# 13 in place of 16 of the 31 convolution taps on ScalarE and GpSimd, with a third buffer for them

## The chip, the cores and the metric

The kernel runs on one core of a Trainium2 chip. Its engines are TensorE (PE in the profile; PEld is its loading of weights), VectorE (DVE), ScalarE (ACT), GpSimd (POOL) and SyncE (SP), which here only issues DMAs. Each engine takes its instructions from a queue of its own, in order; semaphores tie the queues together. The metric is the device time of one execution in microseconds (us); less is better.

## The reference

One layer of a hybrid decoder over 1024 tokens of 1024 numbers, all in float32. Half of the mixer is dilated attention in 8 heads, the other half a gated causal convolution; both go through one output projection. Then an expert layer (PEER) picks 128 of 16384 single-neuron experts for each token, and a gated embedding and a norm follow. Cut to the part that the change touches:

```python
z = xn @ w_in
q, k, v, a, gt = jnp.split(z, [D_ATTN, 2 * D_ATTN, 3 * D_ATTN, 3 * D_ATTN + D_CONV], axis=-1)
...
glu = a * jax.nn.sigmoid(gt)
c = lax.conv_general_dilated(glu, conv_w[:, None, :], window_strides=(1,),
                             padding=[(CONV_WIDTH - 1, 0)],
                             dimension_numbers=('NWC', 'WIO', 'NWC'),
                             feature_group_count=D_CONV) + conv_b
c = jax.nn.silu(_layernorm(c, conv_ln_g, conv_ln_b))
y = jnp.concatenate([_rmsnorm(attn, g_attn_out), _rmsnorm(c, g_conv_out)], axis=-1)
return y @ w_out
```

The convolution is depthwise: each of its 512 channels (`D_CONV`) is the sum of 31 earlier values of that channel (`CONV_WIDTH`), each times a weight of its own, plus a bias.

## The kernel before

The 1024 tokens lie in eight blocks of 128, and the mixer works on four groups of two blocks (256 tokens), g = 0 to 3. For each group it computes the normed input and its projections (`stage_in`), the attention and then the convolution (`stage_attend`), the output projection and the norm of the expert layer (`stage_out`), the search for the experts' keys (`stage_search`) and the combination of these into the best 128 with their gates (`stage_combine`). Blocks 0, 1, 6 and 7 then fetch their experts row by row: GpSimd issues an indirect DMA (L596), VectorE forms the product with the token for the first table (`hk`, L609) and the weighted sum for the second (`gy`, L625). These steps run spread over the whole kernel. Blocks 2 to 5 instead sweep all 128 keys on PE (`dense`, L741 to L776), after the mixer of all groups; the embedding and the last norm end the kernel. A scheduler with priorities and its own estimate of costs interleaves all this: the order of each engine's queue is not the order of the code, and a change in one place can move instructions of others.

The convolution of a group is `convolve` (L323 to L360). Its 512 channels are four tiles, c = 0 to 3, with channels on partitions and 256 tokens along them. For each tile PE forms the gate `gt` and the value `a` (L270), ScalarE the sigmoid `sg` of the gate (L331), and VectorE their product `glu` (L335), with the last 30 values of the group before it in front (L334, L337). `glu` has three buffers, so tile 3 takes that of a tile that is done. Then come the 31 taps. The first `SIDE_TAPS` go to two engines: ScalarE multiplies the shifted `glu` by the weight, the first time into `side` (L346), then into a buffer `tap` (L349), and GpSimd adds each `tap` to `side` (L350). The others go to VectorE: L353 writes the first into a sum in PSUM, `cs`, with the bias, and L356 does one multiply-add for each further tap. At last VectorE adds the two sums into `cc` (L358). `side` has two buffers, so tiles 2 and 3 begin when `cc` of tiles 0 and 1 is done; in the queues VectorE takes the taps of tiles 0 and 1 in turn, then those of 2 and 3. PE transposes `cc` back to tokens (`pc`, L423), and the layer norm of the convolution, its share of `mixed`, and the output projection follow. In names such as `cs2_3` the first number is the group, the second the channel tile; `tap1_0_14` is tap 14 of group 1, tile 0.

Other names in the rows: `r_mix` (L153) is the factor of the norm of the next group's input, `xt` (L286) its scaled input, which PE transposes (`pt_mix`, L162); `pT` (L164) is ScalarE's copy of transposed probabilities of the attention, `po` its product; `ge`, `tmp`, `step` (L557 to L566, halved in L544 to L551) belong to the combination and are bf16; `ya` is the output of the attention, `sqj_ya` its sum of squares on ScalarE.

Of the kernel before, what the change touches and what calls it, by code (L numbers as in the profile page):

```python
# [10 lines left out]
F32 = mybir.dt.float32  # L11
# [9 lines left out]
P = 128  # L21
# [8 lines left out]
GN = GT * P  # L30
# [7 lines left out]
DC = 512  # L38
NCT = DC // P
TAPS = 31  # L40
SIDE_TAPS = 16
ROT = 8
PH = 8
TOPK = 16
# [57 lines left out]
def tile_layer(ctx, tc, t, consts, out):  # L102
# [18 lines left out]
    def scope(parent, **kw):  # L121
        s = parent.enter_context(ExitStack())
        return s, s.enter_context(tc.tile_pool(bufs=1, **kw))
# [8 lines left out]
    att, apool = scope(ctx, name="apool", side="right")  # L132
# [132 lines left out]
    def channel_major(xT, w_k, c0, name):  # L265

        w = w_piece(w_k[c0], f"w_{name}").rearrange("p (k c) -> p k c", k=KD)
        a = lin(name)[:, : xT.shape[2]]
        for k in range(KD):
            nc.tensor.matmul(a, w[:, k, :], xT[:, k, :], start=k == 0, stop=k == KD - 1)  # L270
        return a
# [52 lines left out]
    def convolve(g, xT):  # L324

        gn = xT.shape[2]
        glus = []
        for c in range(NCT):
            pg = channel_major(xT, w_ag, NCT + c, f"gt{g}_{c}")
            sg = mpool.tile([P, GN], F32, tag="t2", name=f"sg{g}_{c}", bufs=3)[:, :gn]  # L330
            S.activation(sg, pg, AF.Sigmoid)  # L331
            pa = channel_major(xT, w_ag, c, f"a{g}_{c}")
            glu = apool.tile([P, TAPS - 1 + GN], F32, tag="glu", name=f"glu{g}_{c}", bufs=NCT - 1)[:, : TAPS - 1 + gn]
            V.tensor_copy(glu[:, 0 : TAPS - 1], last[:, c, :])  # L334
            V.tensor_tensor(glu[:, TAPS - 1 :], pa, sg, ALU.mult)  # L335
            if g + 1 < NG:
                V.tensor_copy(last[:, c, :], glu[:, gn:])  # L337
            glus.append(glu)
        cT = []
        for c, glu in enumerate(glus):  # L340
            tap = lambda k: (glu[:, k : k + gn], cw[:, c, k : k + 1])
            side = apool.tile([P, GN], F32, tag="side", name=f"side{g}_{c}", bufs=2)[:, :gn]
            for k in range(SIDE_TAPS):
                xk, wk = tap(k)
                if k == 0:
                    S.activation(side, xk, AF.Copy, scale=wk)  # L346
                else:
                    m = apool.tile([P, GN], F32, tag="tap", name=f"tap{g}_{c}_{k}", bufs=2)[:, :gn]
                    S.activation(m, xk, AF.Copy, scale=wk)  # L349
                    G.tensor_tensor(side, side, m, ALU.add)  # L350
            sums = lin(f"cs{g}_{c}")[:, :gn]
            xk, wk = tap(SIDE_TAPS)
            V.tensor_scalar(sums, xk, wk, cw[:, c, TAPS : TAPS + 1], ALU.mult, ALU.add)  # L353
            for k in range(SIDE_TAPS + 1, TAPS):
                xk, wk = tap(k)
                V.scalar_tensor_tensor(sums, xk, wk, sums, ALU.mult, ALU.add)  # L356
            cc = apool.tile([P, GN], F32, tag="cc", name=f"cc{g}_{c}", bufs=5)[:, :gn]
            V.tensor_tensor(cc, sums, side, ALU.add)  # L358
            cT.append(cc)
        return cT  # L360
# [474 lines left out]
    def stage_attend(g):  # L835
        qT, xT = st[g]
        ys = attend(g, qT)
        st[g] = (ys, convolve(g, xT))
# [143 lines left out]
```

## Time and profile before

| | us |
|---|---|
| Median of 3 runs | 3184.26 |
| Lowest and highest | 3178.24, 3186.3 |
| Profiled execution | 3174.52 |
| Span of its instructions | 3172.8 |
| PE busy | 2723.0 |
| VectorE busy | 2487.8 |
| GpSimd busy | 1551.7 |
| ScalarE busy | 1154.2 |

The profile is of one execution. Its span runs from the first to the last instruction; the execution's own time is 1.7 us longer. "Busy" counts the time in which an engine had an instruction in work. The mean TensorE clock granted over the span was 0.939 of full speed. By stretches of time, the four mixers fill the first 1040 us, the work of the last group's search and combination follows, and the sweep over all keys runs from about 1455 to 3050 us.

A line of the timeline gives when a run of equal instructions starts, how long it lasts, the engine, the line of the code, the operation, what is written and read, the shapes and the number of instructions. In brackets stands how long the engine was idle before it and which instruction ended that idle time.

### The profile page before, as it was taken

What the parts mean: (1) busy time and instruction counts of PE and PEld (TensorE: products, weight loads), DVE (VectorE), ACT (ScalarE), POOL (GpSimd) and SP (SyncE); (2) the same over time, 40 slices, a digit from 0 to 9 for tenths busy, and PEclk for the clock granted to TensorE, in tenths of its full rate; (3) what the DMA queues carried; (4) which work ended last, traced back from release to release, by engine and by line L of the source; (5) the groups of instructions that cost most, each with busy time, mean ns of one, the idle gap of its engine ahead of it and who ended that gap; (6) DMA issues with size and microseconds to landing.
All of it is one profiled execution on the core that took longest, in us unless ns stands there. A gap on an engine that the chain in (4) does not pass through costs nothing. (4 is left out here: it accounts for less than half of the span.)

```text
span 3172.8 us, 36112 instructions
## 1 busy us (share of the span) xinstructions
PE 2723.0 (86%) x11711; PEld 1994.6 (63%) x11711; DVE 2487.8 (78%) x5116; ACT 1154.2 (36%) x2129; POOL 1551.7 (49%) x1268
## 2 busy tenths in 40 slices
PE   6588938986995677996999999999999999999996
PEld 3455614853574365665777777777777777777643
DVE  1428867997897799886889889888888888888851
ACT  3623453264345327882222222222222222232342
POOL 0500685466546531215556556566556566655620
PEclk9799969988998788997999999999999999999998
DMA  5154849845954664989999999999999999999840
GB/s 164 54 168 135 313 161 376 313 159 196 354 199 153 255 255 129 283 264 346 339 338 331 332 339 361 342 347 343 334 331 346 343 339 361 335 329 333 324 169 24
DMA packets 304528, 865.76 MB, mean 273 GB/s; under 512 B 26778, under 2 KB 93746, under 8 KB 304338
## 3 DMA queue, kind: packets, MB, share of 16 engines
q0 software_dynamic: 147456, 536.94, 46.4%
q1 hardware_dynamic: 153616, 323.16, 29.4%
q10 hardware_dynamic: 3266, 3.36, 0.4%
q8 instruction: 92, 1.51, 0.2%
q14 instruction: 98, 0.80, 0.1%
HBM read 819.83 MB, written 43.52 MB: 272 GB/s over the span
## 5 line engine op out<-in xcount | busy, mean ns | idle before, releaser
L596 POOL DMA_INDIRECT u<-in_expert_u_dram,ex x512 | 674.1, 1317 | 812.1 <-DVE hk L609 539.4
L596 POOL DMA_INDIRECT v<-in_expert_v_dram,ex x512 | 692.4, 1352 | 494.7 <-DVE gy L625 362.9
L625 DVE SCALAR_TENSOR_TENSOR gy<-v,ga,gy 128x1024 f32<-128x1024 f32 x512 | 657.5, 1284 | 41.8 <-DMA v<-in_expert_v_dram,ex 33.0
L609 DVE CUSTOM_DVE_ANT_0 u<-u,gxn 128x1024 f32<-128x1024 f32 x512 | 613.7, 1226 | 57.9 <-DMA u<-in_expert_u_dram,ex 57.7
L741 PE MATMUL ph<-xh,uh 128*128 128x512 f32 x1024 | 404.5, 395 | 42.5 <-DMA gt<-gate_d 29.0
L743 PE MATMUL ph<-xh,ul 128*128 128x512 f32 x1024 | 407.2, 398 | 23.6 <-DVE ul L719 23.4
L742 PE MATMUL ph<-xl,uh 128*128 128x512 f32 x1024 | 402.6, 393 | 0.0
L759 ACT CAST vh<-v 128x1024 fp32r<-128x1024 f32 x128 | 131.5, 1051 | 736.8 <-PE kept_y L774 491.2
L350 POOL TENSOR_TENSOR side<-side,tap 128x256 f32<-128x256 f32 x240 | 184.9, 771 | 183.6 <-ACT tap L349 135.1
L741 PEld LDWEIGHTS ph<-xh,uh 128*128 128x128 f32 x1024 | 194.5, 190 | 89.2 <-ACT uh L717 49.8
L743 PEld LDWEIGHTS ph<-xh,ul 128*128 128x128 f32 x1024 | 194.1, 190 | 79.3 <-DVE ul L719 39.3
L772 PE MATMUL py<-vh,ah 128*128 128x512 f32 x512 | 204.4, 399 | 43.8 <-ACT ah L751 43.8
L761 DVE TENSOR_TENSOR vl<-v,vh 128x1024 fp32r<-128x1024 f32 x128 | 153.8, 1222 | 110.2 <-ACT vh L759 110.1
L270 PE MATMUL pq<-x2T,w_pq 128*128 128x256 f32 x1024 | 230.4, 383 | 5.7 <-DMA w_pq<-in_peer_wq_dram 5.3
L742 PEld LDWEIGHTS ph<-xl,uh 128*128 128x128 f32 x1024 | 194.5, 190 | 41.7
L270 PEld LDWEIGHTS pq<-x2T,w_pq 128*128 128x128 f32 x1024 | 193.7, 192 | 34.6 <-issue 4.5
L773 PE MATMUL py<-vl,ah 128*128 128x512 f32 x512 | 200.4, 395 | 0.0
L774 PE MATMUL kept_y<-vh,al 128*128 128x512 f32 x512 | 199.4, 390 | 0.0
L772 PE MATMUL kept_y<-vh,ah 128*128 128x512 f32 x512 | 199.3, 389 | 0.0
L773 PE MATMUL kept_y<-vl,ah 128*128 128x512 f32 x512 | 199.2, 389 | 0.0
L774 PE MATMUL py<-vh,al 128*128 128x512 f32 x512 | 198.8, 395 | 0.0
L717 ACT CAST uh<-u 128x1024 fp32r<-128x1024 f32 x128 | 134.1, 1048 | 108.0 <-DMA u<-in_uT_dram 78.9
(264 smaller groups left out, 4685.2 us busy)
## 6 DMA issues: line engine op xcount, KB each, us to landing
u<-in_uT_dram SPq DMA_DIRECT2D x128, 512.0 KB, 6.9
v<-in_expert_v_dram SPq DMA_DIRECT2D x128, 512.0 KB, 6.5
w_pq<-in_peer_wq_dram SPq DMA_DIRECT2D x64, 512.0 KB, 5.8
gate_d<-stage SPq DMA_DIRECT2D x16, 2048.0 KB, 11.5
gt<-gate_d SPq DMA_DIRECT2D x64, 512.0 KB, 10.8
w_o<-in_w_out_dram SPq DMA_DIRECT2D x32, 512.0 KB, 5.8
w_k<-in_w_qkv_dram SPq DMA_DIRECT2D x16, 512.0 KB, 5.0
w_q<-in_w_qkv_dram SPq DMA_DIRECT2D x16, 512.0 KB, 4.3
```

What stands on the lines that cost most here:

```text
L270: nc.tensor.matmul(a, w[:, k, :], xT[:, k, :], start=k == 0, stop=k == KD - 1)
L350: G.tensor_tensor(side, side, m, ALU.add)
L596: d = G.indirect_dma_start(out=e, out_offset=None, in_=table, in_offset=bass.IndirectOffsetOnAxis(ap=index, axis=0))
L609: uses(V.tensor_tensor_reduce(out=e, in0=e, in1=xn, scale=1.0, scalar=0.0, op0=ALU.mult, op1=ALU.add, accum_out=hk[:, k : k + 1]))
L625: uses(V.scalar_tensor_tensor(y, e, act[:, k : k + 1], y, ALU.mult, ALU.add))
L741: nc.tensor.matmul(ph, hi, xh[:, k, :], start=k == 0, stop=False)
L742: nc.tensor.matmul(ph, hi, xl[:, k, :], start=False, stop=False)
L743: nc.tensor.matmul(ph, lo, xh[:, k, :], start=False, stop=k == KD - 1)
L761: V.tensor_tensor(b, v, a.bitcast(F32), ALU.subtract)
L772: nc.tensor.matmul(py, ah[e][:, rows(j)], vh[e][:, half(f)], start=first, stop=False)
L773: nc.tensor.matmul(py, ah[e][:, rows(j)], vl[e][:, half(f)], start=False, stop=False)
L774: nc.tensor.matmul(py, al[e][:, rows(j)], vh[e][:, half(f)], start=False, stop=last_e)
```

## The change

`SIDE_TAPS` goes from 16 to 13, the buffers of `tap` from two to three, and those of `cc` from five to four. For each channel tile ScalarE now multiplies 13 taps and GpSimd adds 12; VectorE takes 18, one by L353 and 17 by L356, where it was 15, one and 14. Each `tap` and each `cc` buffer holds 256 float32 numbers per partition, so the two pools together need as much memory as before.

```diff
-SIDE_TAPS = 16
+SIDE_TAPS = 13
...
-                    m = apool.tile([P, GN], F32, tag="tap", name=f"tap{g}_{c}_{k}", bufs=2)[:, :gn]
+                    m = apool.tile([P, GN], F32, tag="tap", name=f"tap{g}_{c}_{k}", bufs=3)[:, :gn]
...
-            cc = apool.tile([P, GN], F32, tag="cc", name=f"cc{g}_{c}", bufs=5)[:, :gn]
+            cc = apool.tile([P, GN], F32, tag="cc", name=f"cc{g}_{c}", bufs=4)[:, :gn]
```

The counts alone do not tell the order of the queues, which the scheduler makes anew. Three places differ in more than the number of taps.

The first is VectorE at the end of the convolution of group 2. Before, the queue held:

```order
L356 SCALAR_TENSOR_TENSOR cs2_3_4204<-glu2_3_3958,cw_91,cs2_3_4204 128x256
L358 TENSOR_TENSOR cc2_2_4155<-cs2_2_4139,side2_2_4092 128x256
L356 SCALAR_TENSOR_TENSOR cs2_3_4204<-glu2_3_3958,cw_91,cs2_3_4204 128x256
L563 TENSOR_TENSOR tmp2_4289<-ge2_4283,step2_4286 128x2048
L356 SCALAR_TENSOR_TENSOR cs2_3_4204<-glu2_3_3958,cw_91,cs2_3_4204 128x256
L544 TENSOR_TENSOR tmp2_4289<-tmp2_4289 128x128x8
L356 SCALAR_TENSOR_TENSOR cs2_3_4204<-glu2_3_3958,cw_91,cs2_3_4204 128x256
L566 TENSOR_TENSOR ge2_4283<-ge2_4283,cb16_87 128x2048
L358 TENSOR_TENSOR cc2_3_4220<-cs2_3_4204,side2_3_4157 128x256
L544 TENSOR_TENSOR ge2_4283<-ge2_4283 128x128x8
L153 RECIPROCAL r_mix3_4415<-sd_mix3_4413 128x2
L153 RECIPROCAL r_ya2_4617<-sd_ya2_4615 128x2
```

and now it holds:

```order
L356 SCALAR_TENSOR_TENSOR cs2_2_4070<-glu2_2_3882,cw_91,cs2_2_4070 128x256
L356 SCALAR_TENSOR_TENSOR cs2_3_4129<-glu2_3_3910,cw_91,cs2_3_4129 128x256
L358 TENSOR_TENSOR cc2_2_4089<-cs2_2_4070,side2_2_4032 128x256
L358 TENSOR_TENSOR cc2_3_4148<-cs2_3_4129,side2_3_4091 128x256
L557 TENSOR_TENSOR ge2_4211<-ge2_4211,cb16_87 128x2048
L153 RECIPROCAL r_mix3_4343<-sd_mix3_4341 128x2
L153 RECIPROCAL r_ya2_4545<-sd_ya2_4543 128x2
L563 TENSOR_TENSOR tmp2_4217<-ge2_4211,step2_4214 128x2048
L334 COPY glu3_0_5683<-last_100 128x30
L334 COPY glu3_1_5710<-last_100 128x30
L544 TENSOR_TENSOR tmp2_4217<-tmp2_4217 128x128x8
```

The operations of the combination (`tmp2`, `ge2`), which lay between the last taps of tile 3, now come behind `cc2_3`; one of them, L557, lies between it and `r_mix3`.

The second is ScalarE in the convolution of group 1, where tiles 0 and 1 end. Before, these rows stood among the taps of tiles 0 and 1:

```order
L349 ACTIVATE tap1_0_14_2368<-glu1_0_2239,cw_91 128x256
L151 ACT_TABLE_LOAD
L151 ACTIVATE sd_mix2_2596<-ssq_mix2_2591,eps_89 128x2
L349 ACTIVATE tap1_0_15_2371<-glu1_0_2239,cw_91 128x256
L349 ACTIVATE tap1_1_1_2394<-glu1_1_2267,cw_91 128x256
L146 ACTIVATE sqj_ya1_0_2794,ssq_ya1_2793<-ya2_2071 128x512
L349 ACTIVATE tap1_1_2_2397<-glu1_1_2267,cw_91 128x256
L349 ACTIVATE tap1_1_3_2400<-glu1_1_2267,cw_91 128x256
L146 ACTIVATE sqj_ya1_1_2796,ssq_ya1_2793<-ya3_2213 128x512
L349 ACTIVATE tap1_1_4_2403<-glu1_1_2267,cw_91 128x256
L349 ACTIVATE tap1_1_5_2406<-glu1_1_2267,cw_91 128x256
L151 ACTIVATE sd_ya1_2798<-ssq_ya1_2793,eps_89 128x2
```

and `side1_2` came later, right behind the last of those taps and the first two of tile 2. Now the same operations follow the last tap of tile 1:

```order
L349 ACTIVATE tap1_1_11_2394<-glu1_1_2243,cw_91 128x256
L349 ACTIVATE tap1_1_12_2397<-glu1_1_2243,cw_91 128x256
L349 ACTIVATE tap1_2_1_2423<-glu1_2_2271,cw_91 128x256
L349 ACTIVATE tap1_2_2_2426<-glu1_2_2271,cw_91 128x256
L349 ACTIVATE tap1_2_3_2429<-glu1_2_2271,cw_91 128x256
L151 ACT_TABLE_LOAD
L151 ACTIVATE sd_mix2_2548<-ssq_mix2_2543,eps_89 128x2
L146 ACTIVATE sqj_ya1_0_2746,ssq_ya1_2745<-ya2_2047 128x512
L146 ACTIVATE sqj_ya1_1_2748,ssq_ya1_2745<-ya3_2189 128x512
L151 ACTIVATE sd_ya1_2750<-ssq_ya1_2745,eps_89 128x2
L346 ACTIVATE side1_2_2421<-glu1_2_2271,cw_91 128x256
L346 ACTIVATE side1_3_2480<-glu1_3_2299,cw_91 128x256
```

The table load, `sd_mix2`, the two `sqj_ya1` and `sd_ya1` now lie between the last tap of tile 1 and `side1_2`.

The third is ScalarE in the convolution of group 3, around the last sigmoid `sg3_3`. Before:

```order
L349 ACTIVATE tap3_1_12_5939<-glu3_1_5782,cw_91 128x256
L349 ACTIVATE tap3_1_13_5942<-glu3_1_5782,cw_91 128x256
L349 ACTIVATE tap3_1_14_5945<-glu3_1_5782,cw_91 128x256
L331 ACTIVATE sg3_3_5823<-gt3_3_5814 128x256
L146 ACTIVATE sqj_ya3_0_6283,ssq_ya3_6282<-ya6_5467 128x512
L146 ACTIVATE sqj_ya3_1_6285,ssq_ya3_6282<-ya7_5729 128x512
```

and now, where tile 1 had its last taps between the heads of the attention (`sb7` and `pT7` are those of block 7):

```order
L349 ACTIVATE tap3_1_12_5861<-glu3_1_5710,cw_91 128x256
L386 ACTIVATE sb7_7_5623,den7_5398<-sb7_7_5623,nm7_7_5624 128x1024
L164 COPY pT7_6_4_5612<-pt_p7_6_4_0_5613 128x512
L331 ACT_TABLE_LOAD
L331 ACTIVATE sg3_2_5724<-gt3_2_5715 128x256
L164 COPY pT7_7_0_5633<-pt_p7_7_0_0_5634 128x512
L556 COPY ge4_6064<-p164_6062 128x2048
L164 COPY pT7_7_4_5644<-pt_p7_7_4_0_5645 128x512
L349 ACTIVATE tap3_2_1_5887<-glu3_2_5737,cw_91 128x256
L349 ACTIVATE tap3_2_2_5890<-glu3_2_5737,cw_91 128x256
L349 ACTIVATE tap3_2_3_5893<-glu3_2_5737,cw_91 128x256
L331 ACTIVATE sg3_3_5751<-gt3_3_5742 128x256
```

The taps 4 to 14 of `tap3_1`, which stood in one row between the last `pT7` copy and `sg3_3` (the last three are shown), have moved ahead among the copies; three taps of tile 2 stand ahead of `sg3_3` now. On VectorE the combination's `tmp4` and the three operations that follow it (L544, L566, L544) come behind `cc3_3`, where before they lay ahead of the taps.

## Rows read from the trace of the kernel before

**Rows 1.** The page's first part: busy us (share of the span) and instructions by engine.
```profile
PE 2723.0 (86%) x11711; PEld 1994.6 (63%) x11711; DVE 2487.8 (78%) x5116; ACT 1154.2 (36%) x2129; POOL 1551.7 (49%) x1268
```

**Rows 2.** Busy us (instructions) by stretch: PE, PEld, DVE, ACT, POOL; clock, DMA share, GB/s.
```profile
700.00:738.00 38.00, 0.17 (x1) 0.00 (x0) 28.33 (x71) 21.01 (x43) 25.43 (x32) 0.54 0.14 51
...
1098.00:1170.00 72.00, 68.28 (x330) 57.85 (x330) 62.20 (x252) 11.56 (x27) 35.45 (x28) 0.97 0.87 328
...
1455.00:2950.00 1495.00, 1414.90 (x6058) 1139.98 (x6058) 1309.24 (x1720) 400.44 (x514) 894.33 (x640) 0.99 0.93 338
...
3051.00:3173.00 122.00, 89.91 (x230) 44.43 (x228) 21.26 (x33) 34.31 (x70) 0.00 (x0) 0.86 0.09 33
```

**Rows 3.** Tile `side`: durations in ns (min/median/max), then who waited: us, times.
```profile
L350 POOL TENSOR_TENSOR side<-side,tap x240: 716/725/1802, 91.4 to 1038.1; 128x256 f32<-128x256 f32 x120
...
  ACT tap L349: 78.0, 179
...
  DVE cc L358: 51.9, 9
```

**Rows 4.** Tile `cs`: what its engine sat idle for: us, times.
```profile
  ACT sg L331: 15.4, 3
```

**Rows 5.** Timeline, first convolution: start us, duration us, operation, [idle before <-releaser].
```profile
104.27 16.71 POOL L350 TENSOR_TENSOR side<-side,tap 128x256 f32<-128x256 f32 x21 [1.64 <-ACT tap L349]
...
112.64 3.62 PE L270 MATMUL gt<-xT,w_gt 128*128 128x256 f32 x16
...
121.82 0.55 DVE L353 TENSOR_SCALAR cs<-glu,cw 128x256 f32<-128x256 f32 x1 [6.80 <-ACT sg L331]
...
134.69 23.89 POOL L350 TENSOR_TENSOR side<-side,tap 128x256 f32<-128x256 f32 x30 [13.71 <-ACT side L346]
...
158.61 0.42 DVE L358 TENSOR_TENSOR cc<-cs,side 128x256 f32<-128x256 f32 x1 [11.48 <-POOL side L350]
```

**Rows 6.** Timeline, second convolution.
```profile
402.12 1.28 ACT L151 ACT_TABLE_LOAD   x1
...
406.10 0.61 ACT L146 ACTIVATE sqj_ya<-ya 128x512 bf16<-128x512 f32 x1
...
416.94 0.42 DVE L358 TENSOR_TENSOR cc<-cs,side 128x256 f32<-128x256 f32 x1 [6.41 <-POOL side L350]
...
417.92 23.86 POOL L350 TENSOR_TENSOR side<-side,tap 128x256 f32<-128x256 f32 x30 [1.02 <-ACT side L346]
...
418.17 11.05 DVE L356 SCALAR_TENSOR_TENSOR cs<-glu,cw,cs 128x256 f32<-128x256 f32 x28
...
429.91 0.42 DVE L358 TENSOR_TENSOR cc<-cs,side 128x256 f32<-128x256 f32 x1 [0.69 <-POOL side L350]
...
441.82 0.42 DVE L358 TENSOR_TENSOR cc<-cs,side 128x256 f32<-128x256 f32 x1 [11.48 <-POOL side L350]
...
443.55 1.12 PE L162 MATMUL pt_mix<-cst,xt 128*128 128x128 f32 x4 [47.01 <-ACT xt L286]
```

**Rows 7.** Timeline, third convolution.
```profile
710.40 26.14 POOL L350 TENSOR_TENSOR side<-side,tap 128x256 f32<-128x256 f32 x30 [8.75 <-ACT side L346]
...
723.12 1.22 DVE L563 TENSOR_TENSOR tmp<-ge,step 128x2048 bf16<-128x2048 bf16 x1
...
737.51 0.16 DVE L153 RECIPROCAL r_mix<-sd_mix 128x2 f32<-128x2 f32 x1
...
738.90 1.12 PE L162 MATMUL pt_mix<-cst,xt 128*128 128x128 f32 x4 [38.73 <-ACT xt L286]
```

**Rows 8.** Timeline, fourth convolution.
```profile
990.88 3.62 PE L270 MATMUL gt<-xT,w_gt 128*128 128x256 f32 x16
...
991.85 9.42 POOL L350 TENSOR_TENSOR side<-side,tap 128x256 f32<-128x256 f32 x9
...
1002.11 0.55 DVE L353 TENSOR_SCALAR cs<-glu,cw 128x256 f32<-128x256 f32 x1 [5.79 <-ACT sg L331]
```

**Rows 9.** The page's fifth part, the gather's second half: xcount | busy us, mean ns | idle.
```profile
L625 DVE SCALAR_TENSOR_TENSOR gy<-v,ga,gy 128x1024 f32<-128x1024 f32 x512 | 657.5, 1284 | 41.8 <-DMA v<-in_expert_v_dram,ex 33.0
```

## The prediction, made before the change was run

> **What bounds the kernel now.** I began with busy time by engine [rows 1]. TensorE leads with 86%, VectorE has 78%, GpSimd 49%, ScalarE 36%: no engine sets the end alone, so the next view is busy time by stretch [rows 2]. From 1455 to 2950 us, the sweep over all keys, PE is busy 1414.90 of 1495.00 us at a granted clock of 0.99; 3051 to 3173 is PE's tail. Both are PE's, and no convolution lies in them: all sixteen channel tiles (four groups of tokens, four tiles each) are done by 1039 us. In that front part PE waits. In 700 to 738 us it works 0.17 of 38.00 us, at a mean clock of 0.54 (near the lower of its levels, 1.2 of 2.4 GHz), while VectorE works 28.33 and GpSimd 25.43. That stretch is the end of a convolution.
>
> The third view is who waits for the side sums [rows 3]: VectorE stood idle 51.9 us in nine places, before adding `side` to its own sum, until GpSimd's last add. The tile of VectorE's sums shows a second wait, 15.4 us in three places, for the sigmoid `sg` on ScalarE [rows 4]. These are what the change can reach; the rest of the front waits for other things.
>
> The fourth view is the timeline at the four convolutions. VectorE does tiles 0 and 1 together ("pair 1"), then 2 and 3 ("pair 2"). In pair 2 of the second convolution GpSimd's 30 adds take 23.86 us, 0.795 each, and VectorE's 28 fused taps 11.05 us, 0.395 each [rows 6]. VectorE then waits 11.48 us, PE waits with it, and the transposes of the next group come only behind it, after 47.01 us of idle PE. Here a tap taken from GpSimd costs half as much on VectorE, and VectorE has the room. Is ScalarE the limit instead? No: its multiplies are shorter than an add, and the 30 adds stand in one unbroken row. So the third `tap` buffer, and the ScalarE time saved, are worth nothing in pair 2.
>
> **The change part by part.** GpSimd loses 3 adds in each of 16 tiles: 48 x 0.795 = 38.2 us. ScalarE loses 48 multiplies. VectorE gains 48 taps: 48 x 0.395 = 19.0 us. Of that, 24 taps lie in the four pairs 2, under GpSimd, which needs 24 x 0.795 = 19.1 us there against about 14.4 for VectorE (34 x 0.395 and two first taps). Thus each pair 2 shortens by 6 x 0.795 = 4.8 us and VectorE keeps some 4.5 us of idle time. What pair 1 does differs by convolution.
>
> First convolution [rows 5]. In pair 1 VectorE waits 6.80 us for the sigmoid of tile 3, which stands on ScalarE among the taps of tile 1, and these run at GpSimd's pace: GpSimd's 21 adds end at 104.27 + 16.71 = 120.98. With six adds fewer they end at 104.27 + 15 x 0.796 = 116.2. The gate's product is on PE until 112.64 + 3.62 = 116.26, so the sigmoid cannot start before that, and VectorE's start moves from 121.82 to about 117.2: 4.6 us earlier, less 6 x 0.395 = 2.4 for its own added taps, 2.2 net. With pair 2, **-6.9** (rounded down from 7.0).
>
> Second convolution [rows 6]. Pair 1 ends with a wait of 6.41 us for GpSimd, at 416.94. GpSimd's adds would end 4.8 us earlier or more; VectorE's own taps end 2.4 later, at about 412.4, so the end is about 412.8, 4.1 earlier. But the order on ScalarE changes: the table load, the norm of the next tokens and the two of `ya` (1.28 us and three or four pieces of 0.3 to 0.6) come behind pair 1's last tap, ahead of `side1_2`, where before they lay among the taps. I take 2 us late from it. 4.1 + 4.8 - 2 = **-7.1** (bounds -6 and -9).
>
> Third convolution [rows 7]. Pair 2's 30 adds take 26.14 us, not 23.9, because three operations of the search's combination on two bf16 inputs (1.22 us for `tmp`, and two like it) run on VectorE beside them. After the change they stand behind the last `cc`, but for one of 1.2 us ahead of `r_mix3`. The pair starts 0.5 us later (2.4 for its own taps, less what the shorter tile 0 gives back), takes 19.1, and pays the 1.2: 710.9 + 19.1 + 0.4 + 1.2 = 731.8 for `r_mix3` against 737.5, **-5.7**. At the worst VectorE, which has the 3 to 4 us of deferred work and 2.4 of taps still to do, gives all but 0.4 of it back in the next stage; at best -7.
>
> Fourth convolution [rows 8]. Before, the sigmoid of tile 3 stood behind eleven taps of tile 1, and VectorE waited 5.79 us, starting at 1002.11; the gate's product ends on PE at 994.5. In the new order those taps lie earlier, between the heads of the attention, so VectorE may start at about 995.0. 34 x 0.395 then puts pair 1's end 4.6 us earlier; pair 2 gives 4.8: -9.4. Two costs stand against it. ScalarE's copies of the probabilities (`pT7`) now have up to three taps between them and PE waits for those copies: twelve taps of 0.5 us, mostly in gaps, for which I take +2 (bounds 0 and +10, if each tap waits for its add behind a gather fetch). And four bf16 operations (3.8 us) with three more gather steps (3 x 1.28 = 3.9 [rows 9]) reach VectorE between this convolution and the sweep; from 1040 on VectorE has idle time (62.20 of 72.00 busy in 1098 to 1170 [rows 2]), so I take +2.5 of at most +7.7. Sum **-4.9**.
>
> Sweep and tail: 0, since PE sets both [rows 2] and nothing in its work there changes; a few gather steps move by two places under 1309.24 us of VectorE. The fifth buffer of `cc` goes, and costs nothing: a group has four, and the next group's first comes 150 us or more after its transposes.
>
> The sum is -6.9 - 7.1 - 5.7 - 4.9 = -24.6 us. The profiled execution took 3174.52 us, 1.7 more than its span and 9.7 under the median of the runs shown, 3184.26. 3174.52 - 24.6 = 3149.9; on the median, 3159.7, which I call **3159**.
>
> One rule speaks against the change. In pair 2 of the second convolution the first 15 adds ran beside VectorE's taps (417.92 to 429.91, 12.0 us) and the last 15 while VectorE stood idle (to 441.82, 11.9 us) [rows 6]: the taps do not slow GpSimd. The third convolution's adds beside bf16 operations did slow, to as much as 1.80 us [rows 3, 7]. The Trainium skill, "SBUF — State Buffer", section "Who interferes with whom", says that a VectorE instruction with two SBUF inputs contends with a GpSimd instruction that reads SBUF, and one with at most one SBUF input does not. The taps have one input in SBUF and one in PSUM, the bf16 operations two in SBUF, and the trace agrees on both. By that rule the taps that move are free of contention, and my sum would stay.
>
> **The rivals.**
>
> *GpSimd's adds slow down* (slower). After the change VectorE works through 14.4 of pair 2's 19.1 us, before 12.0 of 23.9. If more of VectorE's work beside them stretches the adds, as in the nine adds of 9.42 us at 991.85 (1.047 each [rows 8]), pair 2 takes 24 x 1.047 = 25.1 us, 1.2 longer than now; with 2.4 on VectorE in pair 1 that is +3.6 in each convolution, +14.4 in all: about **3199**. It decides from 0.896 us per add ((23.9 - 2.4) / 24). Against it stands the equal pace of the two halves above. The Trainium skill's "Perfetto Trace Analysis", section "Optimizing Scalar/DVE Operations", advises the opposite of this change (work off a saturated VectorE, on to ScalarE or even GpSimd); with VectorE idle in pair 2 the trace does not bear that out. Chance 0.05.
>
> *The gain is lost behind the convolutions* (little change). Attention 7 is held up by the taps among its copies (+10 in place of +2), the deferred work of the fourth convolution lies wholly on the path (+7.7 in place of +2.5), and the third gives back all but 0.4. Then -24.6 + 8 + 5.2 + 5.3 = -6.1: about **3178**, within the noise. For it speaks that VectorE is the busiest engine around these places; against it, that 28.33 of 38.00 us in the third tail leave it idle time. Chance 0.14.
>
> *The third buffer gives more.* In pairs 1 of the third and fourth convolutions adds alternate with gather fetches, and ScalarE's queue, which also holds PE's copies, waits for adds. With a tap more of slack ScalarE stands less often: -35 to -40, about **3147**. Nothing in the rows prices it beyond the 78 us that ScalarE waited in all. Chance 0.15.
>
> *It does not do what it says.* If the convolution's end did not release PE, nothing would move: 3184. The wait of 11.48 us before the last `cc`, with PE idle for 47.01 us and released by the instruction behind it [rows 6], speaks against it. Chance 0.02.
>
> **How the numbers follow.** Forecast (about -13 to -33 us) 0.64, more gain 0.15, lost gain 0.14, slower 0.05, nothing 0.02. The range leaves out the slower rival, the flat cases' far end and the far end of the large gain: 3143 to 3176. A measurement of this kernel can tell 0.3%, about 9.5 us, from no change. Faster by more than that: 0.64 + 0.15 = 0.79 and a little of the lost-gain case, 0.80. Within it: 0.14, less that, and 0.02: 0.15. Slower: 0.05.
>
> **What would show it.** In the new trace VectorE's wait for GpSimd before `cc` should fall from 51.9 us to about 18 (four times 4.5); the wait for the sigmoid from 15.4 to a few; pair 2 should be an unbroken row of 24 adds in 19.1 us; the idle PE before the transposes of the next tokens should fall from 47.01 by about 7 and in the third convolution from 38.73; and the sweep should keep its length of 1495 us but start near 1430. I am wrong if adds take over 0.9 us in pair 2, if attention 7 grows by more than the fourth convolution gives, or if the sweep or PE's tail changes by more than 5 us.

## The result and the profile after

The changed kernel took 3154.72 us (median of 4 runs, 3145.36 to 3160.1) against 3185.28 us for the kernel before (4 runs beside it). That is 30.6 us faster; the forecast was 3159 with a range of 3143 to 3176. The ratio of the runs on record is 0.9912, interval 0.9889 to 0.9935 (that of the two medians is 0.9904). Three later comparisons, on two chips, gave 0.9936 (0.9918 to 0.9955), 0.9963 (0.995 to 0.9976) and 0.9938 (0.9916 to 0.9961): the change gains 0.4 to 0.9%, some 20 us in the mean of the four. Single executions of the changed kernel spread from 3145 to 3178 us. The profiled one took 3160.1 us, so the difference of two profiled executions (14.4 us) says less than the stages in them.

The busy time of the changed kernel, against [rows 1]:

```profile
PE 2740.0 (87%) x11711; PEld 2003.6 (63%) x11711; DVE 2504.5 (79%) x5164; ACT 1132.6 (36%) x2082; POOL 1487.7 (47%) x1220
```

VectorE has 16.7 us more in 48 more instructions, GpSimd 64 us less. Next, who waits around the tiles `side` and `cs` (durations in ns; then us, times), against [rows 3, 4]:

```profile
L350 POOL TENSOR_TENSOR side<-side,tap x192: 718/727/1803, 91.0 to 1011.0; 128x256 f32<-128x256 f32 x192
...
  DVE cc L358: 21.2, 4
...
  ACT sg L331: 8.3, 2
```

VectorE's wait for GpSimd fell from 51.9 us in nine places to 21.2 in four, its wait for the sigmoid from 15.4 to 8.3. The timeline of the first convolution (start us, duration us, operation, [idle before <-releaser]), against [rows 5]:

```profile
117.47 0.55 DVE L353 TENSOR_SCALAR cs<-glu,cw 128x256 f32<-128x256 f32 x1 [3.59 <-ACT sg L331]
...
132.69 19.12 POOL L350 TENSOR_TENSOR side<-side,tap 128x256 f32<-128x256 f32 x24 [16.07 <-ACT side L346]
...
133.30 13.40 DVE L356 SCALAR_TENSOR_TENSOR cs<-glu,cw,cs 128x256 f32<-128x256 f32 x34
...
151.84 0.42 DVE L358 TENSOR_TENSOR cc<-cs,side 128x256 f32<-128x256 f32 x1 [4.82 <-POOL side L350]
```

Pair 1 starts at 117.47, where it was 121.82. Pair 2 is one unbroken row of 24 adds in 19.12 us beside 34 taps in 13.40; VectorE still waits 4.82 us, not 11.48. The second convolution, against [rows 6]:

```profile
406.88 0.41 DVE L358 TENSOR_TENSOR cc<-cs,side 128x256 f32<-128x256 f32 x1
...
408.32 0.61 ACT L146 ACTIVATE sqj_ya<-ya 128x512 bf16<-128x512 f32 x1
...
409.83 19.10 POOL L350 TENSOR_TENSOR side<-side,tap 128x256 f32<-128x256 f32 x24 [4.16 <-ACT side L346]
...
428.97 0.43 DVE L358 TENSOR_TENSOR cc<-cs,side 128x256 f32<-128x256 f32 x1 [6.71 <-POOL side L350]
...
430.70 1.11 PE L162 MATMUL pt_mix<-cst,xt 128*128 128x128 f32 x4 [41.32 <-ACT xt L286]
```

Pair 1 no longer waits for GpSimd. Pair 2's first add waits 4.16 us for `side1_2`, which stands behind the two `sqj_ya` on ScalarE; the idle PE before the transposes fell from 47.01 to 41.32 us. The third and the fourth, against [rows 7, 8]:

```profile
699.68 19.10 POOL L350 TENSOR_TENSOR side<-side,tap 128x256 f32<-128x256 f32 x24 [15.12 <-ACT side L346]
...
718.81 0.42 DVE L358 TENSOR_TENSOR cc<-cs,side 128x256 f32<-128x256 f32 x1 [4.79 <-POOL side L350]
...
721.68 1.12 PE L162 MATMUL pt_mix<-cst,xt 128*128 128x128 f32 x4 [31.93 <-ACT xt L286]
...
973.70 3.24 PE L270 MATMUL gt<-xT,w_gt 128*128 128x256 f32 x14
...
976.98 0.38 ACT L331 ACTIVATE sg<-gt 128x256 f32<-128x256 f32 x1 [2.45 <-issue]
...
992.62 19.11 POOL L350 TENSOR_TENSOR side<-side,tap 128x256 f32<-128x256 f32 x24 [14.45 <-ACT side L346]
...
1011.76 0.42 DVE L358 TENSOR_TENSOR cc<-cs,side 128x256 f32<-128x256 f32 x1 [4.89 <-POOL side L350]
```

The last `cc` starts at 1011.76 us. Before, it was this row:

```profile
1038.90 0.42 DVE L358 TENSOR_TENSOR cc<-cs,side 128x256 f32<-128x256 f32 x1 [11.48 <-POOL side L350]
```

27.1 us are gained there, and 14.4 of them reach the end of the program. How the stages compare in all the traces of the two programs, each stage in us from one mark of the timeline to the next (the start of the last `cc` of each convolution, the start of the first product of the sweep on L741, the end of its last product on L774, the start of the last instruction, which issues the output's DMA):

| Stage | Before, 2 traces | Changed, 4 traces | Difference of means | Forecast |
|---|---|---|---|---|
| to the first convolution's end | 158.6, 159.8 | 151.8, 153.4, 152.4, 153.7 | -6.4 | -6.9 |
| to the second's | 283.2, 284.6 | 277.1, 276.1, 274.3, 274.1 | -8.5 | -7.1 |
| to the third's | 294.8, 294.2 | 289.8, 291.9, 290.9, 283.7 | -5.4 | -5.7 |
| to the fourth's | 302.3, 304.4 | 293.0, 303.2, 298.1, 300.3 | -4.7 | -7.4 |
| to the sweep | 416.0, 418.7 | 426.2, 423.3, 422.8, 428.1 | +7.7 | +2.5 |
| sweep | 1515.8, 1519.2 | 1519.4, 1518.1, 1522.6, 1523.3 | +3.4 | 0 |
| tail | 198.4, 198.4 | 197.3, 195.9, 198.2, 197.6 | -1.1 | 0 |

The gains of the first three convolutions and the loss behind the fourth stand in every trace. The stage to the fourth convolution spreads over 10 us in one program. All of that spread lies ahead of the last taps: from the end of the last gate product on PE (before 990.88 + 3.62 = 994.50, changed 973.70 + 3.24 = 976.94) to the last `cc` it takes 44.4 us in both traces of before and 34.8 in all four of the changed kernel.

### The profile page after: what moved, and what is told of

Its sections match the earlier page's. It is cut to its first block, busy times and chain, and to the rows that moved or that the text cites. A ratio compares the mean times of both kernels' runs of the same rounds, so it can differ in the third digit from the quotient of the medians.

```text
span 3158.3 us, 36012 instructions
## 1 busy us (share of the span) xinstructions
PE 2740.0 (87%) x11711; PEld 2003.6 (63%) x11711; DVE 2504.5 (79%) x5164; ACT 1132.6 (36%) x2082; POOL 1487.7 (47%) x1220
## 5 line engine op out<-in xcount | busy, mean ns | idle before, releaser
L596 POOL DMA_INDIRECT u<-in_expert_u_dram,ex x512 | 654.4, 1278 | 830.1 <-DVE hk L609 568.0
L596 POOL DMA_INDIRECT v<-in_expert_v_dram,ex x512 | 682.3, 1333 | 513.0 <-DVE gy L625 380.6
L741 PE MATMUL ph<-xh,uh 128*128 128x512 f32 x1024 | 407.1, 398 | 44.0 <-ACT uh L717 43.9
L741 PEld LDWEIGHTS ph<-xh,uh 128*128 128x128 f32 x1024 | 195.8, 191 | 91.8 <-ACT uh L717 51.9
L350 POOL TENSOR_TENSOR side<-side,tap 128x256 f32<-128x256 f32 x192 | 150.8, 787 | 194.6 <-ACT tap L349 133.6
L742 PEld LDWEIGHTS ph<-xl,uh 128*128 128x128 f32 x1024 | 195.9, 191 | 42.0
L774 PE MATMUL kept_y<-vh,al 128*128 128x512 f32 x512 | 199.7, 390 | 0.0
L774 PE MATMUL py<-vh,al 128*128 128x512 f32 x512 | 198.3, 395 | 0.3 <-DVE al L753 0.3
```

Of the source, the lines that this page charges most:

```text
L596: d = G.indirect_dma_start(out=e, out_offset=None, in_=table, in_offset=bass.IndirectOffsetOnAxis(ap=index, axis=0))
L741: nc.tensor.matmul(ph, hi, xh[:, k, :], start=k == 0, stop=False)
L742: nc.tensor.matmul(ph, hi, xl[:, k, :], start=False, stop=False)
L774: nc.tensor.matmul(py, al[e][:, rows(j)], vh[e][:, half(f)], start=False, stop=last_e)
```

## The experiments

**Was the first pair of traces chance?** Both kernels as they are, once more each.

> The changed kernel once more, for a second trace and a narrower ratio. In the first pair of traces the four convolutions ended 27.1 us earlier, but the program only 14.4 us earlier: 10.1 us went between the last convolution and the sweep, where the output projection of the last group waited for its weights (w_o) by DMA. Theory 1 (the loss belongs to the new order: three more gather steps, each with a fetch of 512 KB, lie in that stage): this trace shows the same loss, the last cc about 27 us earlier than before and the sweep's first product 16 to 18 us earlier; ratio 0.990 to 0.993. Theory 2 (the loss was chance of one execution, since the medians lie 30 us apart): the sweep starts 22 to 28 us earlier than before.

> The kernel before once more, for a second trace: how far the times of the stages (last cc, first and last product of the sweep, end) differ between two executions of one program. If the stages repeat within 2 us up to the sweep, and the sweep itself differs by several us, the spread of the runs (3178 to 3188) is made in the sweep, not in the convolutions.

Measured: ratio 0.9936 and, in the second trace of before, 1043.05 us for the last `cc` and 1461.77 for the sweep's first product. The stages of before repeat within 2.7 us up to the sweep, where I had expected 2, and within 3.5 in it. The changed kernel's second trace has the loss behind the fourth convolution again (423.3), so the loss belongs to the new order, as theory 1 has it; which part of the order makes it is asked below. The other numbers of theory 1 missed: against the second trace of before the last `cc` came 18.5 us earlier and the sweep 13.8, not 27 and 16 to 18. The last `cc` came at 1024.59, not 1011.76, and 10 us of that lie in the stage to the fourth convolution, in the attention of the last group. Busy us (instructions) by stretch (PE, PEld, DVE, ACT, POOL; clock, DMA share, GB/s), first of the first trace:

```profile
909.00:918.50 9.50, 8.35 (x46) 5.71 (x47) 9.50 (x54) 7.28 (x16) 8.23 (x10) 1.00 0.04 12
...
918.30:927.30 9.00, 9.00 (x54) 6.40 (x54) 8.62 (x66) 5.21 (x11) 2.84 (x4) 1.00 0.23 65
```

and of the second, for the same work:

```profile
913.00:922.50 9.50, 8.57 (x46) 5.52 (x44) 9.50 (x54) 7.26 (x17) 7.85 (x9) 1.00 0.09 34
...
923.00:940.10 17.10, 17.10 (x53) 11.85 (x54) 8.98 (x66) 6.13 (x12) 2.86 (x4) 0.50 0.18 57
```

The order is the same and PE is full in both, but the same products take 9.00 us in the first trace and 17.10 in the second, where PE runs at its lower level (0.50, 1.2 of 2.4 GHz). That is 8 of the 10 us. Just before it the two traces are alike: PE was busy 8.35 and 8.57 of 9.50 us at 1.00. Of the twelve other traces of this study, four have such a stretch with PE full in this attention (10 to 17 us), and one, that of the taps alone (below), has 10.2 us with PE busy in 9.50 of them; the changed kernel's third and fourth and the two of before have none. What brings it on stays open.

**Which part of the change works?** The taps alone and the buffers alone.

```diff
# taps_only, against the kernel before
-SIDE_TAPS = 16
+SIDE_TAPS = 13
# buffer_only, against the changed kernel
-SIDE_TAPS = 13
+SIDE_TAPS = 16
```

> 13 side taps, with two tap buffers and five cc buffers as before. If the gain is GpSimd's three fewer adds in each tile, and the third buffer is worth nothing: pair 2 is 24 adds of 0.796 us, the last cc of the fourth convolution 23 to 28 us earlier than before, and the time equals the changed kernel's within 0.3%. Here VectorE's queue keeps the combination's bf16 operations inside the third convolution, which costs 2 to 3 us there, but only 18 gather steps lie between the last convolution and the next norm, as before, not 21, so that the loss in that stage should be smaller by theory 1: sweep 20 to 28 us earlier. If the third buffer carries the gain (ScalarE waits less for adds): 10 us or less faster than before.

> 16 side taps as before, with three tap buffers and four cc buffers. If the buffer is worth nothing in itself: 30 adds still take 23.9 us in pair 2 and the time is within 0.3% of before. The order of VectorE's queue changes with it (two of the bf16 operations leave the third convolution), which may give 2 us there. If the buffer carries the gain: 15 us or more faster.

Measured, beside the changed kernel's 0.9936 on the same chip: taps alone 0.9961 (0.9941 to 0.998), buffers alone 1.0032 (1.0015 to 1.005), some 10 us slower than before, which neither expectation had. With 13 taps the third buffer adds some 7 us of gain (the intervals overlap, so this is likely and not settled), with 16 it costs 10. It does nothing to the adds: 24 of them took 19.07 us with two buffers. With taps alone the last `cc` came at 1031.90, 7.0 and 11.1 us earlier than in the two traces of before, not 23 to 28: in this trace the attention of the last group took longer (10.2 us of it at the lower clock), and a wait is back. What the buffer changes is the order. The fourth convolution with taps alone:

```profile
997.17 0.36 ACT L331 ACTIVATE sg<-gt 128x256 f32<-128x256 f32 x1
...
997.57 0.55 DVE L353 TENSOR_SCALAR cs<-glu,cw 128x256 f32<-128x256 f32 x1 [5.79 <-ACT sg L331]
...
1012.80 19.07 POOL L350 TENSOR_TENSOR side<-side,tap 128x256 f32<-128x256 f32 x24 [14.97 <-ACT side L346]
```

Here nine multiplies of tile 1 stand ahead of `sg3_3` on ScalarE, as eleven did before the change, and VectorE waits 5.79 us for it, as in [rows 8]. In the changed kernel they lie among the attention's heads and that wait is gone. The sweep came 417.2 us behind the last `cc`, as in before: 21 gather steps lie there up to the first product of the next search, 22 in before, 25 in the changed kernel. With the buffers alone the order is disturbed too, and to no use:

```profile
422.25 23.90 POOL L350 TENSOR_TENSOR side<-side,tap 128x256 f32<-128x256 f32 x30 [4.16 <-ACT side L346]
...
714.91 24.99 POOL L350 TENSOR_TENSOR side<-side,tap 128x256 f32<-128x256 f32 x30 [9.88 <-ACT side L346]
...
727.67 1.22 DVE L557 TENSOR_TENSOR ge<-ge,cb 128x2048 bf16<-128x2048 bf16 x1
...
1029.82 25.00 POOL L350 TENSOR_TENSOR side<-side,tap 128x256 f32<-128x256 f32 x30 [14.44 <-ACT side L346]
```

In the second convolution the first add waits 4.16 us for a `side1_2` that the same ScalarE work precedes as in the changed kernel, and no shorter pair pays for it. VectorE no longer waits for the last sigmoid here either. The rest of this trace's loss lies mostly in the last group's attention, where 20 us run at the lower clock, which by the 17.10 and 9.00 us above costs some 10 (an estimate). One trace does not explain a median of twelve runs; their granted clock was lower as well, 0.9335 in the mean against 0.9372 in the 23 runs of before beside them, and what lowers it is not shown. The two buffer counts were always changed together, so the runs do not tell them apart.

**Where do the 8 us behind the last convolution go?** The gather's steps on VectorE held back there, with their fetches.

```diff
-        V.reciprocal(r, sd)
+        marks[name] = V.reciprocal(r, sd).ins.name
...
-            uses(V.scalar_tensor_tensor(y, e, act[:, k : k + 1], y, ALU.mult, ALU.add))
+            uses(gy := V.scalar_tensor_tensor(y, e, act[:, k : k + 1], y, ALU.mult, ALU.add)); order_after(gy.ins, marks["ffn3"]) if (i, k) == (FEW[0], 104) else None
```

> The changed kernel, in which the 104th row of the first gathered block is used on VectorE only after the norm behind the last output projection (r_ffn3): five gather steps lie between the last convolution and that norm, not 21, and the fetches of 512 KB behind them wait too. All else keeps its order up to the last cc. If the gain of the convolutions is lost in that stage to the gather's rows, which share the DMA engines with the weights w_o: from the last cc to the sweep's first product 410 to 416 us, in place of 426 and 423, and the time 6 to 14 us under the changed kernel's. If the loss comes from VectorE's deferred bf16 operations or from a lower clock by chance: the stage stays at 420 or more and the time is the same. If the gather's rows are on the path anyway: the sweep and its tail get longer by what the stage gains, and the time is the same.

The output projection of the last group, from the last `cc` to the first product of the search, in before, in the changed kernel and in this one:

```profile
1039.00:1099.40 60.40, 41.00 (x102) 19.47 (x103) 53.52 (x79) 22.71 (x41) 27.52 (x21) 0.81 0.73 258
```

```profile
1011.80:1084.40 72.60, 47.00 (x102) 21.10 (x103) 61.62 (x86) 22.83 (x41) 29.75 (x24) 0.78 0.70 249
```

```profile
1024.40:1081.50 57.10, 41.34 (x102) 19.31 (x103) 44.12 (x71) 22.83 (x41) 11.22 (x8) 0.83 0.55 183
...
1081.50:1444.40 362.90, 288.07 (x1642) 208.01 (x1641) 300.21 (x797) 215.74 (x518) 88.01 (x79) 0.88 0.74 239
```

60.40, 72.60 and 57.10 us, with 22, 25 and 10 gather steps. PE's waits in it, in the changed kernel and in this one:

```profile
1047.92 1.98 PE L261 MATMUL o<-w_o,yT 128*128 128x512 f32 x4 [2.64 <-DMA w_o<-in_w_out_dram]
...
1052.42 2.70 PE L261 MATMUL o<-w_o,yT 128*128 128x512 f32 x4 [2.52 <-DMA w_o<-in_w_out_dram]
...
1067.48 5.24 PE L261 MATMUL o<-w_o,yT 128*128 128x512 f32 x8 [3.79 <-DMA w_o<-in_w_out_dram]
```

```profile
1041.56 3.39 PE L261 MATMUL o<-w_o,yT 128*128 128x512 f32 x4 [3.96 <-DMA w_o<-in_w_out_dram]
...
1051.33 19.35 PE L261 MATMUL o<-w_o,yT 128*128 128x512 f32 x42
```

One wait for the weights `w_o` is left, of 3.96 us; behind it 42 products run in one row. VectorE's bf16 operations, which this kernel has in the same place, do not make the stage long by themselves: the gather's steps are needed for it. But holding them back takes two things out of the stage at once, VectorE's time for them (busy 44.12 us, not 61.62) and their fetches (183 GB/s, not 249), so this run does not tell which of the two costs. The other traces, between the same two marks, do not settle it either (us; the last column is PE's waits for `w_o`):

| Kernel | Gather steps | Stage | VectorE busy | `w_o` waits |
|---|---|---|---|---|
| before, 2 traces | 22 | 60.4, 62.2 | 53.5, 53.8 | 7.0, 5.9 |
| taps alone | 21 | 59.9 | 53.2 | 5.5 |
| changed, 4 traces | 25 | 72.6, 70.5, 69.8, 69.1 | 61.7 in each | 8.9, 9.6, 10.6, 11.3 |
| steps held back | 10 | 57.1 | 44.1 | 4.0 |
| buffers alone | 20 | 64.9 | 53.0 | 10.5 |
| 11 taps (below) | 19 | 63.8 | 51.6 | 10.7 |
| 9 taps (below) | 19 | 67.6 | 51.5 | 8.4 |
| 16 taps in the fourth (below) | 20 | 65.7 | 53.1 | 10.8 |

From before to the changed kernel VectorE's busy time grew by 8 us, and the stage by 9; PE's waits for weights grew by some 4. The last four kernels have fewer steps than before and no more work on VectorE, and yet they wait longer for weights and take longer. So the number of steps alone does not set it. They share the third `tap` buffer with the changed kernel, and with it another order; what in that order delays the weights stays open.

The stage behind, up to the sweep, takes 362.90 us here, against 353.6 in the changed kernel's first trace (352.9 to 359.1 in the others), and the time is 0.9932 (0.99 to 0.9963), the changed kernel's within the noise. The whole came out at 420 us, not at the 410 to 416 of the first expectation. The steps held back take their time further on, as in the third expectation, but ahead of the sweep and not in the sweep and its tail, where I had put it.

**Is 13 the best number, and when does VectorE become the bound?** `SIDE_TAPS` 11 and 9, the rest as changed.

> 11 side taps, three tap and four cc buffers. Pair 2: GpSimd 20 x 0.796 = 15.9 us, VectorE 38 x 0.395 and two first taps and a cc = 16.4 us, so that both end together; 3 us less than with 13. Pair 1: 4 x 0.395 = 1.6 us more on VectorE. Net 1.4 us less in each convolution, and 15 gather steps, not 21, in the last output projection, worth some 5 us: 5 to 11 us faster than the changed kernel. If VectorE is already the bound of the front with 13: 16 to 25 us slower than it (64 taps more at 0.395 over both).

> 9 side taps. Pair 2 is now bound by VectorE: 42 x 0.395 + 1.4 = 18.0 us, GpSimd 16 x 0.796 = 12.7; 1.5 us less than with 13 taps. Pair 1: 8 x 0.395 = 3.2 us more. Net +1.7 in each convolution, +7 in all, less some 5 us for 15 gather steps in the last output projection: 0 to 7 us slower than the changed kernel, and 5 to 12 slower than with 11 taps. VectorE does not wait for GpSimd before any last cc. If fewer side taps always pay: faster than with 11.

Measured: 0.9941 (0.9919 to 0.9964) and 0.9969 (0.9947 to 0.9991); the changed kernel's four ratios, on other occasions, have a mean of 0.9937. So the 5 to 11 us that I expected from 11 taps did not come. Pair 2 of the first convolution with 11 and with 9:

```profile
135.10 15.89 POOL L350 TENSOR_TENSOR side<-side,tap 128x256 f32<-128x256 f32 x20 [18.07 <-ACT side L346]
...
135.71 14.97 DVE L356 SCALAR_TENSOR_TENSOR cs<-glu,cw,cs 128x256 f32<-128x256 f32 x38
...
150.59 0.86 DVE L358 TENSOR_TENSOR cc<-cs,side 128x256 f32<-128x256 f32 x2
```

```profile
136.32 12.65 POOL L350 TENSOR_TENSOR side<-side,tap 128x256 f32<-128x256 f32 x16 [21.26 <-ACT side L346]
...
136.93 16.54 DVE L356 SCALAR_TENSOR_TENSOR cs<-glu,cw,cs 128x256 f32<-128x256 f32 x42
...
153.37 0.75 DVE L358 TENSOR_TENSOR cc<-cs,side 128x256 f32<-128x256 f32 x2
```

With 11 both engines end together, and neither kernel has a wait of VectorE for GpSimd left: the forecast of pair 2 (15.9 and 16.4, 12.7 and 18.0) was right. With 9 VectorE is the bound, and the median lies 4.7 us above that with 11, as expected, though the intervals overlap. With 11 the convolutions' gain did not reach the time: in the fourth, six multiplies of tile 1 stand ahead of `sg3_3` again, which costs VectorE a wait of 4.44 us, and the stage to it took 307.5 us.

**Is the fourth convolution worth its gain?**

```diff
-SIDE_TAPS = 13
+SIDES = (13, 13, 13, 16)
...
-            for k in range(SIDE_TAPS):
+            for k in range(SIDE_TAPS := SIDES[g]):
```

> 13 side taps in the first three convolutions, 16 in the fourth. The last cc should come 7 to 10 us later than in the changed kernel. If its gain is given back through the gather steps of the stage behind it (16 steps there, not 21): 5 to 8 us of that come back and the time is 0 to 4 us over the changed kernel's. If the loss has another cause: 8 to 10 us slower than the changed kernel.

Measured: 0.9979 (0.9957 to 1.0), some 13 us over the changed kernel's mean. The stage behind the last `cc` is shorter, 419.5 us against 425.1, as expected; but the last `cc` came at 1030.87, 15 us over the changed kernel's mean of 1015.9. Only 4.1 of these are the convolution's own: from the last gate product to the last `cc` this trace takes 38.9 us, where the changed kernel takes 34.8. The attention ahead takes most of the rest, some 5 of it in a stretch of 10.2 us at the lower clock; with 16 taps three more multiplies of each tile of pair 1 stand among its copies, as with buffers alone. So the run changes two things, and does not say how much of the convolution's own gain is given back. My 0 to 4 us was wrong.

**A mix that keeps what the runs showed**: 11 taps in the first two convolutions, 13 in the others.

```diff
-SIDES = (13, 13, 13, 16)
+SIDES = (11, 11, 13, 13)
```

> 11 side taps in the first two convolutions, 13 in the others, three tap and four cc buffers. With 11 taps everywhere the first convolution ended at 151.0 us (13 taps: 151.8 to 153.4) and the second 273.8 us behind it (13 taps: 276.1 to 277.1), but the fourth lost its early sigmoid: eight of ScalarE's multiplies stood ahead of sg3_3 again. This mix keeps the early sigmoid and the 21 gather steps behind the fourth convolution. If the ends of the convolutions add up: last cc 3 to 5 us earlier than in the changed kernel, and the time 2 to 5 us under it on the same chip (ratio to before 0.991 to 0.993). If stages behind give it back: the same time as the changed kernel.

> The changed kernel a third time, beside the mix on one chip. Stages: first convolution ends at 151.8 to 153.4, the second 276 to 277 behind it, from last cc to the sweep's first product 423 to 426 us. The stage between the third and the fourth convolution: 293 us if the clock of TensorE stays at its upper level through the attention, 303 if it falls to the lower one for some 16 us there as in the second trace. Ratio to before 0.990 to 0.995.

> 11, 11, 13 and 13 side taps once more, beside the changed kernel on one chip, since their intervals touched. If the mix is better by what its first two convolutions save: ratio to before 0.990 to 0.995 and 3 to 12 us under the changed kernel; last cc 1008 to 1018 us. If the first comparison was chance: the two within 3 us.

> The changed kernel a fourth time, beside the mix. The three ratios so far were 0.9912, 0.9936 and 0.9963; a ratio of 0.992 to 0.996 agrees with them. First convolution ends at 151.8 to 153.4 us, from last cc to the sweep's first product 422 to 427.

Measured, chip by chip: 3160.05 against 3172.36 us for the changed kernel (ratios to before 0.993 [0.9908 to 0.9953] and 0.9963 [0.995 to 0.9976]), then 3164.73 against 3170.72 (0.9927 [0.99 to 0.9954] and 0.9938 [0.9916 to 0.9961]). The mix is clearly faster than the kernel before and lies under the changed one both times, by 12 and 6 us, but the intervals overlap, so that its lead is likely and not settled. In its second convolution both engines end pair 2 together:

```profile
410.14 15.87 POOL L350 TENSOR_TENSOR side<-side,tap 128x256 f32<-128x256 f32 x20 [8.29 <-ACT side L346]
...
425.63 0.83 DVE L358 TENSOR_TENSOR cc<-cs,side 128x256 f32<-128x256 f32 x2
```

The first convolution ends at 150.6 us in both traces, 2.2 earlier than in the changed kernel; the second takes 275.4 and 274.9 us more, as in that one, so only part of the 3 to 5 us that I expected at the last `cc` shows in the stages: it came at 1016.0 and 1011.8 us. Both traces have a stretch at 0.50 in the last attention (10.3 and 13.6 us), which by the same price hides some 5 and 6 us (an estimate). Of the changed kernel's two traces here, the third took 298.1 us to the fourth convolution with the clock at its upper level through the attention, between the 293 and the 303 that I had named, and the fourth 428.1 us from the last `cc` to the sweep, just over my 422 to 427.

## Why the prediction was right, and where its terms were off

**The mechanism was right.** Pair 2 was bound by GpSimd, and each tap moved freed 0.796 us there for 0.395 on VectorE, which had the room: 24 adds in 19.10 to 19.12 us in all four convolutions, as worked out. VectorE's remaining wait is 4.8 us, not 4.5, and 6.7 in the second convolution. Gains of 6.4, 8.5 and 5.4 us for the first three, in the means of the traces, stand against 6.9, 7.1 and 5.7 (6.8, 6.1 and 4.9 in the first pair of traces). Two slips of mine are too small to matter: the sum for `r_mix3` comes to 731.6, not 731.8, and in the second convolution's pair 1 VectorE's taps would end at 416.94 - 6.41 + 2.4 = 412.9, not 412.4; that pair came 3.3 us earlier against the end of the first convolution, not 4.1.

**The slower rival fell.** Adds at 0.896 us or more would have made the change a loss; they kept 0.796 beside 34 taps as beside 28. The Trainium skill, "SBUF — State Buffer", section "Who interferes with whom", says that a VectorE instruction with at most one SBUF input, outside its two-port modes, does not contend with GpSimd, and the trace agrees; with buffers alone, where one bf16 operation of 1.22 us with two SBUF inputs (`ge` from `ge` and `cb16`) lies beside pair 2 of the third convolution, 30 adds took 24.99 us, not 23.9.

**The term that was mis-sized** is the +2.5 us behind the fourth convolution. It measured +7.7, the upper end that I gave it. I charged VectorE's deferred work and three gather steps to VectorE's time, 7.7 us, and took its idle time from 1040 on as cover for most of it. It did not cover that: in the output projection VectorE was busy 8 us longer, and the stage took 9 us more. Whether the steps cost there by this time or by their fetches, while PE's waits for weights grew by some 4 us, no run separates, and neither accounts for the kernels with fewer steps. I had the DMA share of 0.87 in [rows 2] for the stretch behind and did not weigh it. The rival in which the gain is lost behind the convolutions named this place with +7.7; of its other two losses, the third convolution's did not come, and PE's wait for the attention's copies rose by little over 1 us. The sweep therefore started at 1438 us in the first trace, not near 1430.

**The fourth convolution** gave 4.7 us in the mean, not 7.4. Its own part came out as worked out, and in every trace: 44.4 us from the last gate product to the last `cc` before and 34.8 after is -9.6, for the -9.4 of adds and sigmoid. What ate into it lies in the stretch from `cc2_3` to the end of that product: 257.9 and 260.0 us before, 258.1, 268.4, 263.3 and 265.6 changed, which is +4.9 in the mean for my +2. I had charged that to taps among the copies, and PE's wait for the copies did rise, from 0.8 and 1.3 us to 2.1 to 2.8. The larger parts were in no step of mine: 8 us by the clock in the second trace, and PE's waits for the weights `w_o` of the third group, whose output projection runs in the same stretch, 4.5 and 5.8 us in the third and fourth traces against 1.6 and 2.0 before.

**The third buffer** was called worth nothing in pair 2, which holds. But the early sigmoid of the fourth convolution, -4.6 of my -9.4, depends on it: without it the wait of 5.79 us is back. It is not enough by itself, since with 11 taps and the same buffers VectorE waits 4.44 us. The rival of a larger gain through that buffer was right that it matters and wrong in how: it moves the scheduler's order, and ScalarE's slack has no part in it that a run shows.

**The sum** of -24.6 us lies between the stages of the traces (-15.0) and the first measurement (-30.6), and near the mean of the four comparisons (about -20). That the first median fell within 5 us of 3159 is in part luck: the changed kernel's four medians lie from 3154.72 to 3172.36. My 0.3% as what a measurement can tell was too fine for one comparison, as the four ratios of one pair of kernels lie 0.5% apart. Of the signs of being wrong none came in the means of the traces: adds of 0.796 us, an attention that grew by less than the fourth convolution gave, and +3.4 and -1.1 us in sweep and tail.

## What to carry to other kernels

Where two engines share a sum and one waits for the other at the end, the work to move is found by setting their paces equal in that stage (here 11 taps, 15.9 against 16.4 us), not from the busy shares over the whole span. It is a start only, and 11 taps everywhere were no faster here than 13: look in the queue orders of every stage for what else moved. A gain can be partly given back in a later stage: count what the new order puts into it, as time on the busy engine and as bytes for the DMA engines. And a buffer that no wait asks for can still matter, by the order that a scheduler makes with it, so take such parts of a change apart.

## What the runs showed of the hardware

TensorE's granted clock fell to 0.50 for 10 to 17 us in the middle of an attention in which PE was full, in some executions of a program and not in others. In the second trace of the changed kernel the same products took 17.10 us where they had taken 9.00, 8 us of that stage, though PE had been about as busy just before in both (8.35 and 8.57 of 9.50 us). That is a part of why single runs of one kernel spread by over 20 us (3145 to 3178), and a change of 0.6% needs several comparisons. Within a set of runs the time mostly falls as the mean granted clock rises: in the changed kernel's fourth set 3155.15 us came with 0.942 and 3178.02 with 0.936. Which of the two causes the other these numbers do not show.
